# A decoder block with a mixture of experts on one core: the sums of a gate rearranged between VectorE and TensorE, and the loads of a branch's body issued by GpSimd

## The chip, the cores and the metric

The kernel runs on one core of one Trainium2 chip. Times are device microseconds (us) of that core; lower is better. An execution is timed as a whole. A profiled execution has, beside its own time, a span: the time from the first to the last instruction that the profile shows.

The core has five engines with a queue each: TensorE (PE; the profile shows its weight loads apart, as PEld), VectorE (DVE), ScalarE (ACT), GpSimd (POOL) and SyncE (SP), which here only issues transfers. Sixteen DMA engines move what the queues issue.

## What is computed

One block over 256 tokens of width 1024, one sequence, fp32. From a conditioning vector c comes a row of six modulation vectors:

```
mod = silu(c) @ w_ada + b_ada;  sh1, sc1, ga1, sh2, sc2, ga2 = split(mod, 6)     # 1024 each
h = rms_norm(x) * (1 + sc1) + sh1
q, k, v, xb, bg, cg, gates = split(h @ w_in)                                     # 3 x 512, 3 x 512, 2 x 1024
y_a = causal attention(q, k, v);  y_b = bg * (conv3(cg * xb) + b)
x = x + ga1 * ((sigmoid(gate_a) * (y_a @ w_pa) + sigmoid(gate_b) * (y_b @ w_pb)) @ w_o)
h2 = rms_norm(x) * (1 + sc2) + sh2
x = x + ga2 * moe(h2)       # top group of 4, top 2 of its 8 experts; silu(h2 @ w1) * (h2 @ w3) @ w2
```

What the change touches is how ga1 and ga2 (the gates of the two halves of the block), and beside them sh2 and sc2 (the second norm's shift and scale), come to be: each is silu(c) times 1024 columns of w_ada plus a row of b_ada.

## The kernel before

**Two parts.** Up to about 226 us runs the front: modulation, projections, attention, convolution, output. Behind it run the experts, in eight groups of four experts, each 32 tokens at most for an expert; all weights of all experts are loaded, 24 MB a group.

**The stream of weights.** Everything large comes through one list, `stream`, of 1 MB transfers (qkv: 768 KB): first the front's, in the order of `FIRST` and `REST` (L40 to L44; `m2` is a piece of sh2 and sc2, `g1` of ga1, `g2` of ga2, `in` of w_in), then w_pa, w_pb and w_o, then 24 for each group of experts (`in_up_dram`, `in_down_dram`). SyncE issues them strictly in this order (`pump`, L139) into slots: twelve of the ring, two lent by the tiles for the gates, and some more from tiles that are no longer needed late in the front. A transfer waits for the last reader of its slot, and for the transfer eight places before it: these use eight semaphores in turn, `DMAHW0` to `DMAHW7`, which are called lanes here. In the front the last reader of a slot is mostly the instruction that splits it (below), and in the second part the last matmul on it.

**The front's units.** w_in, w_pa, w_pb and w_o are used in 112 units, U0 to U111, each of 128 x 512 weights: U0 to U23 qkv, to U31 cg, to U39 xb, to U47 bg, to U79 the gates, to U95 w_pa and w_pb, to U111 w_o. Each has a split: ScalarE writes the high part (L402), VectorE the low part (L403; GpSimd for U33, U37 and so on to U65), and then TensorE six or twelve matmuls (L434). The splits run three units ahead of the matmuls. The order of the instructions on every engine is the order in which the program is written: `run_units` goes from unit to unit, and behind a unit it takes one step of each side task that is then running. A task is started by `after(unit, task)` and gives up its turn at each `yield` (`yield n` for n units).

**The side tasks of this change.** `mod2_task` (from U34; sh2 and sc2) and `gate2_task` (from U63; ga2) sum on TensorE: a quarter sum (`quarter_sum`, L781) multiplies one column of silu(c) with a 128 x 512 piece and leaves the sum in 32 rows of a PSUM bank, four such sums side by side. mod2's first 16 come behind U34 to U37, its last 16 behind U49 to U52, and then four matmuls (L797) reduce them, with small VectorE operations behind (L794 to L803). `gate1_task` (from U58 for the first 512 columns, from U67 for the others; ga1) sums on VectorE: eight operations on 128 x 512 a half (`ada_sum`, L339) into `part`, which GpSimd has cleared and whose first row it has filled with the bias (`ada_bias`, L343 and L344, from U20 on), and then one matmul with ones (L776) that sums over the 128 rows. The bias of ga2 is added by two matmuls on a loaded row (L811; loaded by GpSimd at L806, from U55 on). Beside these run `attention` (GpSimd multiplies by the reciprocals of its sums at L692 and L693), the convolution (L650), and at U80 and on `pa_task` (L759 to L767), of which L767 writes the low part of the merged branches.

**The branch.** An expert with more than 32 tokens needs extra passes (`alone`). After the third group of experts `overflow` loads the count of the fullest expert into a register and jumps over the body when there is none (L1170). With these inputs the body is jumped over. It is present in the program of each engine that works in it, SyncE among them because the body's weights are loaded through it (L1150, L1159).

## Time and profile before

| | |
|---|---|
| median of three runs | 659.06 us (659.05 to 659.12) |
| the profiled execution, its own time | 660.22 us |
| its span | 658.5 us |
| its mean granted TensorE clock | 0.893 of full speed |
| busy: TensorE, VectorE, ScalarE, GpSimd | 537.1, 194.9, 146.6, 41.5 us |
| moved | 259.01 MB, mean 393 GB/s |

How to read the profile: "busy" is the time in which an engine executes; a wait is idle time before an instruction, put down to what released it ("<-"). L403 is line 403 of the kernel. Names of tiles are the program's, with buffer numbers left out: `slot` is a slot of the ring, `sthi` and `stlo` the high and low parts of a split, `ps` a PSUM bank, `sm` a small tile, `part` and `ada` the accumulators named above. A q behind an engine's name (SPq) is its sequencer, which issues transfers, jumps and waits on semaphores. PEclk is the granted clock of TensorE (1.00 is 2.4 GHz). Transfers are shown from issue to landing.

### The profile page before, as it was taken

The numbers are of one execution on the slowest core, as the hardware profiler recorded it, in microseconds if no ns is written. First come the engines' busy times: TensorE is split into PE (matmuls) and PEld (weight loads), VectorE is DVE, ScalarE is ACT, GpSimd is POOL, SyncE is SP. The second block draws the span as 40 slices with busy tenths as digits, with TensorE's granted clock in tenths as the row PEclk, the third lists the DMA queues.
The fourth block names the chain that finished last, engine by engine and source line by source line (L and its number), as shares of the span: only waits on it lengthen the run. The fifth ranks groups of instructions, "written<-read, shape, count | busy, mean of one in ns | idle before, by whom it ended". The sixth has DMA issues, their size and how long they took to land. (4 is left out here: it accounts for less than half of the span.)

```text
span 658.5 us, 11764 instructions
## 1 busy us (share of the span) xinstructions
PE 537.1 (82%) x5064; PEld 327.5 (50%) x5065; DVE 194.9 (30%) x403; ACT 146.6 (22%) x290; POOL 41.5 (6%) x60
## 2 busy tenths in 40 slices
PE   7999999999999988989585668675976875586666
PEld 6678897878998736354052116201710540061024
DVE  4686539657887412020020001001100100020002
ACT  4536456744555131010010001000000100010001
POOL 0012511600040000000000000000000000000000
PEclk9999999999999998999787888757876596897769
DMA  8999993688959999999999997999999999999997
GB/s 318 425 425 399 426 425 151 258 325 364 417 186 397 411 428 425 425 427 425 427 426 424 425 427 303 425 427 428 425 427 428 426 426 428 426 424 427 428 425 286
DMA packets 37795, 259.01 MB, mean 393 GB/s; under 512 B 4574, under 2 KB 5702, under 8 KB 7272
## 3 DMA queue, kind: packets, MB, share of 16 engines
q1 hardware_dynamic: 36136, 256.98, 94.1%
q10 hardware_dynamic: 1360, 1.05, 0.5%
q8 instruction: 42, 0.69, 0.4%
q0 software_dynamic: 240, 0.16, 0.1%
q14 instruction: 17, 0.14, 0.1%
HBM read 257.12 MB, written 1.05 MB: 392 GB/s over the span
## 5 line engine op out<-in xcount | busy, mean ns | idle before, releaser
L1073 PE MATMUL ps<-slot,xg 128*32 128x512 f32 x1024 | 161.2, 736 | 72.4 <-DMA slot<-in_up_dram 69.1
L1073 PEld LDWEIGHTS ps<-slot,xg 128*32 128x32 f32 x1024 | 26.3, 118 | 190.9 <-DMA slot<-in_up_dram 156.2
L434 PE MATMUL ps<-hbuf,sthi 128*128 128x256 f32 x512 | 94.8, 287 | 0.0
L434 PEld LDWEIGHTS ps<-hbuf,sthi 128*128 128x128 f32 x512 | 79.1, 190 | 11.4 <-ACT sthi L402 6.7
L403 DVE TENSOR_TENSOR stlo<-slot,sthi 128x512 fp32r<-128x512 f32 x100 | 72.0, 723 | 38.8 <-ACT sthi L402 37.8
L402 ACT ACTIVATE sthi<-slot 128x512 fp32r<-128x512 f32 x108 | 67.9, 630 | 63.7 <-PE ps L434 50.0
L1093 PE MATMUL ps<-slot,sl 128*32 128x128 f32 x2048 | 68.1, 288 | 16.4 <-DMA slot<-in_down_dram 11.5
L1081 DVE TENSOR_TENSOR sl<-sl,ps 128x512 f32<-128x512 f32 x8 | 5.5, 687 | 248.1 <-PE ps L1073 241.5
L434 PE MATMUL ps<-hbuf,stlo 128*128 128x256 f32 x256 | 72.2, 282 | 0.7 <-POOL stlo L403 0.7
L1093 PEld LDWEIGHTS ps<-slot,sl 128*32 128x32 f32 x2048 | 57.5, 115 | 30.3 <-DMA slot<-in_down_dram 14.3
L1060 ACT ACTIVATE GW<-ps 128x256 f32<-128x256 f32 x8 | 3.1, 384 | 226.6 <-PE ps L1059 226.6
L1101 PE MATMUL ps<-slot,GW 128*128 128x512 f32 (+1 forms) x76 | 37.4, 620 | 14.3 <-DVE slot L1099 14.3
L434 PEld LDWEIGHTS ps<-hbuf,stlo 128*128 128x128 f32 x256 | 48.5, 190 | 0.9 <-POOL stlo L403 0.9
L434 PE MATMUL ps<-sthi,hbuf 128*128 128x512 f32 x128 | 43.4, 404 | 1.1 <-ACT hbuf L536 0.9
L1040 PEld LDWEIGHTS ps<-GW,x 128*128 128x128 f32 x256 | 35.0, 220 | 7.8 <-issue 6.8
L1040 PE MATMUL ps<-GW,x 128*128 128x128 f32 x256 | 37.6, 310 | 0.6 <-DVE GW L1031 0.6
L1099 DVE TENSOR_TENSOR slot<-ps,slot 128x512 f32<-128x512 f32 (+1 forms) x19 | 11.5, 606 | 87.3 <-PE ps L1093 83.1
L434 PEld LDWEIGHTS ps<-sthi,hbuf 128*128 128x128 f32 x128 | 23.7, 188 | 8.9 <-DVE hbuf L538 1.4
L1101 PEld LDWEIGHTS ps<-slot,GW 128*128 128x128 f32 x76 | 13.7, 210 | 28.4 <-DVE slot L1099 19.2
L1046 ACT ACTIVATE xg<-ps,sm,sm 128x128 f32<-128x128 f32 x32 | 12.4, 457 | 65.9 <-PE ps L1040 65.9
L434 PE MATMUL ps<-stlo,hbuf 128*128 128x512 f32 x64 | 25.1, 392 | 0.0
L1048 DVE TENSOR_SCALAR xg<-ps,sm,sm 128x128 f32<-128x128 f32 x32 | 11.2, 403 | 36.8 <-PE ps L1040 36.8
(263 smaller groups left out, 435.4 us busy)
## 6 DMA issues: line engine op xcount, KB each, us to landing
slot<-in_up_dram SPq DMA_DIRECT2D x128, 1024.0 KB, 19.6
slot<-in_down_dram SPq DMA_DIRECT2D x64, 1024.0 KB, 19.6
slot<-in_front_dram SPq DMA_DIRECT2D x42, 1024.0 KB, 11.6
slot<-in_front_dram SPq DMA_DIRECT2D x8, 768.0 KB, 14.6
gates<-in_front_dram SPq DMA_DIRECT2D x4, 1024.0 KB, 6.9
x<-in_x_dram SPq DMA_DIRECT2D x2, 512.0 KB, 3.7
out_dram<-x ACTq DMA_DIRECT2D x1, 512.0 KB
out_dram<-x ACTq DMA_DIRECT2D x4, 128.0 KB, 1.8
```

The costliest lines, as they stand in the source:

```text
L402: S.activation(hi, src, AF.Copy)
L403: (G if i in on_pool else V).tensor_sub(lo, src, hi.bitcast(F32))
L434: PE.matmul(o, l, r, start=start and n == 0, stop=stop and n == 2, skip_group_check=True)
L1040: PE.matmul(o[:, 128 * (k % 4):128 * (k % 4) + 128], x[:, t, 128 * k:128 * k + 128], Gt[:, t, :], start=t == 0, stop=t == 1)
L1046: S.activation(xg[:, k, :], src, AF.Identity, bias=sh2[:, k:k + 1], scale=a2[:, k:k + 1])
L1048: V.tensor_scalar(xg[:, k, :], src, a2[:, k:k + 1], sh2[:, k:k + 1], op0=OP.mult, op1=OP.add)
L1060: S.activation(WT.rearrange("p t n -> p (t n)"), YC[:, :256], AF.Copy)
L1073: PE.matmul(o[js, :], xg[:, k, js], w[:, j, :], start=k == 0, stop=k == DK - 1)
L1081: V.tensor_mul(sl, sl, HB)
L1093: PE.matmul(bank[js, cs], hidT[:, k, js], w[:, 4 * j + k, :], start=k == 0, stop=k == 3, skip_group_check=True)
L1099: V.tensor_mul(ysb[:, cs], (bank or (YC, YD)[n])[:, cs], ga2[:, ns])
L1101: PE.matmul(ACC[t][n][:, cs], WT[:, t, :], ysb[:, cs], start=q == 0, stop=q == NQ - 1, skip_group_check=True)
```

## The change

- **Order of the stream.** ga1's first pieces (`g100`, `g101`) move forward, between xb and the middle of mod2. The four pieces of ga2 were cut by rows (256 rows x 1024 columns); they are now cut as ga1's (512 rows x 512 columns; `g200`, `g201` for the first 512 columns, `g210`, `g211` for the others).
- **ga1.** Its first half is summed from U37 on (`gate1_sums(0)`) and reduced behind U67; its second is summed from U67 on and reduced behind U76.
- **ga2.** Its first half is summed on VectorE, as ga1 is, from U57 on, into the tile `ada2` that mod2 has used until then; GpSimd clears this tile and loads the bias row into it; one matmul with ones reduces it into bank 1 behind U77. The second half is summed on TensorE by eight quarter sums, in two groups of four (U63 and U75) instead of the sixteen in four groups for both halves before, and its bias (loaded into `part[0]` from U69 on) is added by one matmul behind U86.
- **mod2.** Its second 16 quarter sums start one unit later (`yield 12`).
- **Later.** The squares of the second norm go to bank 7 instead of bank 1, which now holds half of ga2. Behind the first group of experts, one matmul and two copies make ga2's broadcast instead of two matmuls and two copies.
- **The branch.** The body's loads are issued by GpSimd's queue instead of SyncE's.

```
-REST = ("in00 in01 in10 m20 m21 in11 m22 m23 in20 in21 in30 m24 m25 m26 in31 m27 in40 g100 in41 g101 g20 in50 g21 "
-        "g110 in51 g111 g22 in60 g23 in61").split()
+REST = ("in00 in01 in10 m20 m21 in11 m22 m23 in20 in21 g100 in30 g101 m24 m25 m26 in31 m27 in40 g200 in41 g201 in50 "
+        "g210 in51 g110 g111 in60 g211 in61").split()
...
         elif nm[:2] == "g2":
-            i = int(nm[2])
-            f.append((f"ga2.{i}", "w_ada", 256 * i, 2, 512 * GA2, 1024))
+            piece("ada", "w_ada", GA2 + int(nm[2]), int(nm[3]))
...
+    def gate1_sums(half):
+        yield from ada_part(GA1 + half, part[half])
+
     def gate1_task(half, bank):
 
-        p = part[half]
-        yield from ada_part(GA1 + half, p)
-        yield 1
-        PE.matmul(bank, one.to_broadcast([128, 128]), p, start=True, stop=True)
+        PE.matmul(bank, one.to_broadcast([128, 128]), part[half], start=True, stop=True)
         V.tensor_copy(ga1[:, 512 * half:512 * half + 512], bank)
+        yield 1
...
             if k == 3:
                 S.activation(ada2, bank, AF.Copy)
-                yield 11
+                yield 12
...
     def gate2_bias():
-        G.dma_start(ada2[0:2, :], dram("b_ada", 512 * GA2, [[512, 2], [1, 512]]))
+        G.dma_start(part[0][0:1, :], dram("b_ada", 512 * GA2 + 512, [[512, 1], [1, 512]]))
+        yield 1
+
+    def gate2_sums(bank):
+
+        ada_bias(GA2, ada2)
+        yield 1
+        yield from ada_part(GA2, ada2)
+        yield 12
+        PE.matmul(bank, one.to_broadcast([128, 128]), ada2, start=True, stop=True)
 
     def gate2_task(bank):
 
-        for half in range(2):
-            PE.matmul(bank[64 * half:64 * half + 32, :], ident[0:2, half:half + 1].to_broadcast([2, 32]), ada2[0:2, :],
-                      start=True, stop=False, skip_group_check=True)
-        for i in range(4):
-            for kk in range(2):
-                for half in range(2):
-                    quarter_sum(f"ga2.{i}", 2 * i + kk, 2 * kk + half, 2 * half + kk, bank, i == 0 and kk == 1, i == 3)
-            release(f"ga2.{i}")
-            yield 3
+        for i in range(2):
+            for j in range(4):
+                quarter_sum(f"ada11.{i}", 4 * i + j, j, j, bank, i == 0, i == 1 and j > 0)
+            release(f"ada11.{i}")
+            yield 11
+            if i == 0:
+                yield 1
+        PE.matmul(bank[:32, :], one[0:1, :].to_broadcast([1, 32]), part[0][0:1, :], start=False, stop=True,
+                  skip_group_check=True)
...
-    after(58, lambda: gate1_task(0, B[1]))
-    after(67, lambda: gate1_task(1, B[1]))
-    after(55, lambda: iter([gate2_bias()]))
+    after(37, lambda: gate1_sums(0))
+    after(67, lambda: gate1_task(0, B[1]))
+    after(67, lambda: gate1_sums(1))
+    after(76, lambda: gate1_task(1, B[1]))
+    after(56, lambda: gate2_sums(B[1]))
+    after(69, gate2_bias)
     after(63, lambda: gate2_task(B[0]))
...
-                    SY.dma_start(ysb, of_expert("up", e0, 2 * k + m, j))
+                    G.dma_start(ysb, of_expert("up", e0, 2 * k + m, j))
...
-                    SY.dma_start(ysb, of_expert("down", e0, 4 * n + c, j))
+                    G.dma_start(ysb, of_expert("down", e0, 4 * n + c, j))
...
-            for half in range(2):
-                PE.matmul((HA, HB)[half], sel2[:, half:half + 1].to_broadcast([128, 128]), ysb, start=True, stop=True)
-                V.tensor_copy(ga2[:, 512 * half:512 * half + 512], (HA, HB)[half])
+            PE.matmul(HB, sel.to_broadcast([128, 128]), ysb, start=True, stop=True)
+            V.tensor_copy(ga2[:, :512], B[1])
+            V.tensor_copy(ga2[:, 512:], HB)
```

Lines of the changed kernel stand one lower than before's up to about L806, and twelve higher from there on: L403 becomes L402, L339 becomes L338, L1170 becomes L1182.

Where it moves instructions, the orders of three queues show it. The first is SyncE's at the end of the branch: the jump's join (L1170, now L1182) and the transfers behind it, with the semaphores that each waits for. Before:

```order
L1170 UNCONDITIONAL_BRANCH
L1170 UNCONDITIONAL_BRANCH [waits SP_sequencer_49,DMAHW0_49,DMAHW1_49,DMAHW2_49,DMAHW3_49,DMAHW4_49,DMAHW5_49,DMAHW6_49,DMAHW7_49]
L139 DMA slot_79<-in_down_dram 128x2048 [waits DMAHW7_49,PE_49]
L139 DMA slot_85<-in_down_dram 128x2048 [waits DMAHW0_49,PE_49]
L139 DMA slot_83<-in_up_dram 128x2048 [waits DMAHW1_49,PE_49]
```

And the same place now:

```order
L1182 UNCONDITIONAL_BRANCH
L1182 UNCONDITIONAL_BRANCH [waits SP_sequencer_49]
L138 DMA slot_81<-in_down_dram 128x2048 [waits DMAHW7_49,PE_49]
L138 DMA slot_83<-in_down_dram 128x2048 [waits DMAHW0_49,PE_49]
L138 DMA slot_85<-in_up_dram 128x2048 [waits DMAHW1_49,PE_49]
```

The join no longer waits for the eight lanes of the stream; the transfers behind it wait for what they waited for before. SyncE's whole list has 679 rows before and 291 now, since the body's loads have gone to GpSimd.

The second is VectorE's around U58 to U62, where low parts (`stlo`) alternate with the sums of a gate (L339, now L338) and the reciprocals of the attention's sums (L691, now L690). Before:

```order
L403 TENSOR_TENSOR stlo_107<-slot_82,sthi_103 128x512 [waits Activation_49]
L691 RECIPROCAL sm_244<-sm_244 128x8
L403 TENSOR_TENSOR stlo_108<-slot_82,sthi_104 128x512 [waits PE_49,Activation_49]
L403 TENSOR_TENSOR stlo_105<-slot_85,sthi_101 128x512 [waits DMAHW5_49,PE_49,Activation_49]
L691 RECIPROCAL sm_244<-sm_244 128x8
L339 SCALAR_TENSOR_TENSOR part_219<-slot_83,sm_181,part_219 128x512 [waits DMAHW4_49,DMASW0_49]
L403 TENSOR_TENSOR stlo_107<-slot_85,sthi_103 128x512 [waits PE_49,Activation_49]
L339 SCALAR_TENSOR_TENSOR part_219<-slot_83,sm_181,part_219 128x512 [waits DVE_49]
```

Now, with the small operations of mod2 (L794 to L803) one unit later:

```order
L803 SCALAR_TENSOR_TENSOR sm_223<-sm_223,cols_b 128x8 [waits DVE_49]
L690 RECIPROCAL sm_244<-sm_244 128x8
L402 TENSOR_TENSOR stlo_108<-slot_85,sthi_104 128x512 [waits Activation_49]
L402 TENSOR_TENSOR stlo_105<-slot_84,sthi_101 128x512 [waits DMAHW7_49,PE_49,Activation_49]
L690 RECIPROCAL sm_244<-sm_244 128x8
L338 SCALAR_TENSOR_TENSOR ada_202<-slot_86,sm_181,ada_202 128x512 [waits DMAHW6_49,DMASW6_49,Pool_49]
L338 SCALAR_TENSOR_TENSOR ada_202<-slot_86,sm_181,ada_202 128x512 [waits DVE_49]
L402 TENSOR_TENSOR stlo_107<-slot_84,sthi_103 128x512 [waits PE_49,Activation_49]
```

In the place of ga1's first sums stand ga2's, into `ada`; the first of them waits for GpSimd and for one of its loads (DMASW6), and two of them stand ahead of the next low part where one stood before.

The third is GpSimd's around the same units, with the bias row of ga2 and the attention's multiplies (L692 and L693, now L691 and L692; `qkb` for the first half of the heads, `misc` for the second). Before:

```order
L403 TENSOR_TENSOR stlo_106<-slot_82,sthi_102 128x512 [waits DMAHW3_49,PE_49,Activation_49]
L806 DMA ada_202<-in_b_ada_dram 2x512 [waits DVE_49,PE_49]
L692 TENSOR_TENSOR qkb<-qkb,sm_244 128x512 [waits DVE_49]
L693 TENSOR_TENSOR qkb<-qkb,sm_244 128x1024
L692 TENSOR_TENSOR misc<-misc,sm_244 128x512 [waits DVE_49]
L693 TENSOR_TENSOR misc<-misc,sm_244 128x1024 [waits Activation_49]
L403 TENSOR_TENSOR stlo_106<-slot_85,sthi_102 128x512 [waits DMAHW5_49,PE_49,Activation_49]
```

Now:

```order
L402 TENSOR_TENSOR stlo_106<-slot_85,sthi_102 128x512 [waits DMAHW5_49,PE_49,Activation_49]
L691 TENSOR_TENSOR qkb<-qkb,sm_244 128x512 [waits DVE_49]
L692 TENSOR_TENSOR qkb<-qkb,sm_244 128x1024
L342 MEMSET ada_202 128x512 [waits PE_49]
L343 DMA ada_202<-in_b_ada_dram 1x16x32 [waits Pool_49]
L691 TENSOR_TENSOR misc<-misc,sm_244 128x512 [waits DVE_49]
L692 TENSOR_TENSOR misc<-misc,sm_244 128x1024 [waits Activation_49]
L402 TENSOR_TENSOR stlo_106<-slot_84,sthi_102 128x512 [waits DMAHW7_49,PE_49,Activation_49]
```

The load of the bias row stood ahead of all four multiplies; it now stands between those of the two halves, with a clearing of its tile in front of it.

## Rows read from the trace of the kernel before

**Rows 1.** The page: the span; and the span in 40 equal slices, for TensorE the busy share in tenths (9 is 90% or more), and the GB/s that the DMA engines moved.

```profile
span 658.5 us, 11764 instructions
...
PE   7999999999999988989585668675976875586666
...
GB/s 318 425 425 399 426 425 151 258 325 364 417 186 397 411 428 425 425 427 425 427 426 424 425 427 303 425 427 428 425 427 428 426 426 428 426 424 427 428 425 286
```

**Rows 2.** The page's chain of work that ended last, as shares of the span by engine.

```profile
DMA 34%; PE 3%; DVE 0%; issue 0%; ACT 0%; SPq 0%; DVEq 0%
```

**Rows 3.** Stretches of the span. Columns: the stretch and its length in us, the busy us of PE, PEld, DVE, ACT and POOL with the number of instructions, the granted clock of TensorE, the busy share of the DMA engines, GB/s.

```profile
75.00:98.00 23.00, 23.00 (x196) 18.48 (x195) 7.80 (x13) 10.25 (x18) 6.25 (x8) 1.00 1.01 425
98.00:131.00 33.00, 31.30 (x256) 27.13 (x255) 26.09 (x39) 23.37 (x58) 12.91 (x9) 1.00 0.54 214
...
164.00:199.00 35.00, 35.00 (x265) 33.39 (x264) 29.63 (x49) 19.18 (x32) 6.69 (x4) 1.00 0.79 308
199.00:226.00 27.00, 26.79 (x169) 22.91 (x171) 17.93 (x46) 10.68 (x22) 0.00 (x0) 1.00 1.00 404
263.00:395.00 132.00, 98.96 (x1116) 42.64 (x1104) 12.12 (x29) 7.16 (x16) 0.00 (x0) 0.89 1.01 425
411.00:645.00 234.00, 162.77 (x1645) 64.24 (x1634) 15.93 (x33) 10.84 (x24) 0.00 (x0) 0.78 1.01 426
```

**Rows 4.** The waits of SyncE's queue: who waited for what, us in total, times, the longest.

```profile
SPq L139 <- DVE stlo L403: 93.1, 19, 17.6
...
SPq L1170 <- SPq L1170: 18.2, 7, 5.1
...
SPq L139 <- DVE hbuf L767: 3.1, 1, 3.1
```

**Rows 5.** The instructions of line 1170: engine, operation, number, duration in ns (least, median, most), the first and last start in us.

```profile
L1170 SPq EVENT_SEMAPHORE  x9: 17/17/17, 393.7 to 406.9; - x9
...
L1170 POOLq EVENT_SEMAPHORE  x1: 17/17/17, 303.6 to 303.6; - x1
...
L1170 SPq COMPARE_BRANCH  x1: 50/50/50, 388.6 to 388.6; - x1
```

**Rows 6.** The timeline around the branch, from 384 to 396 and from 405 to 410 us: start, us (of several together: from the first to the end of the last), engine, line, operation, and in brackets the idle time before it with what ended it.

```profile
384.85 2.78 SPq L139 DMA_DIRECT2D slot<-in_down_dram  x2
...
406.98 0.69 DVE L1099 TENSOR_TENSOR slot<-ps,slot 128x512 f32<-128x512 f32 x1 [4.18 <-SPq L1170]
407.07 0.81 SPq L139 DMA_DIRECT2D slot<-in_down_dram  x2
...
407.97 2.07 SPq L139 DMA_DIRECT2D slot<-in_up_dram  x4
```

**Rows 7.** The stretch of the hole in DMA, with the columns of the stretches above; then the DMA issues, with KB each and the median us from issue to landing: of the whole span, and of the one issued between 407.9 and 408.4 us.

```profile
401.00:411.00 10.00, 8.22 (x171) 6.59 (x174) 2.06 (x5) 1.51 (x4) 0.00 (x0) 1.00 0.59 226
...
slot<-in_down_dram SPq DMA_DIRECT2D x64, 1024.0 KB, 19.6
...
slot<-in_up_dram SPq DMA_DIRECT2D x1, 1024.0 KB, 10.3
```

**Rows 8.** Groups of TensorE's instructions from 60 to 200 us, forms apart: line, engine, operation, out<-in, forms, number, busy us, mean ns of one, idle before.

```profile
L781 PE MATMUL ps<-slot,sm 128*32 128x512 f32 x88 | 11.7, 604 | 1.0 <-DVE sq L650 1.0
...
L776 PE MATMUL ps<-part,one 128*128 128x512 f32 x4 | 2.0, 590 | 0.0
...
L811 PE MATMUL ps<-ada,ident 2*32 2x512 f32 x4 | 1.0, 599 | 0.0
```

**Rows 9.** All waits of TensorE from 28 to 226 us, and from its timeline the matmul that reads the low part of U62.

```profile
PE ps L781 <- DVE sq L650: 1.0, 1, 1.0
PE ps L434 <- POOL stlo L403: 0.7, 1, 0.7
...
133.70 0.28 PE L434 MATMUL ps<-hbuf,stlo 128*128 128x256 f32 x1
```

**Rows 10.** DMA issues by GpSimd (KB each, median us from issue to landing), and from GpSimd's timeline the clearing of a tile of 128 x 512.

```profile
wr<-in_w_re_dram POOLq DMA_DIRECT2D x1, 128.0 KB, 7.2
part<-in_b_ada_dram POOLq DMA_DIRECT2D x2, 2.0 KB, 5.2
...
ada<-in_b_ada_dram POOLq DMA_DIRECT2D x1, 4.0 KB, 4.7
...
49.65 0.53 POOL L343 MEMSET part<- 128x512 f32 x1 [12.47 <-PE ps L509]
```

**Rows 11.** GpSimd's timeline from 120 to 129 us, the sums of a gate on VectorE (duration in ns: least, median, most; first and last start), and from the page the low parts on VectorE (number | busy us, mean ns of one | idle before).

```profile
120.18 0.57 POOL L806 DMA_DIRECT2D ada<-in_b_ada_dram  x1 [0.54 <-PE ps L797]
121.16 1.04 POOL L692 TENSOR_TENSOR qkb<-qkb,sm 128x512 f32<-128x512 f32 x1 [0.41 <-DVE sm L691]
122.16 1.89 POOL L693 TENSOR_TENSOR qkb<-qkb,sm 128x1024 f32<-128x1024 f32 x1
125.39 1.44 POOL L692 TENSOR_TENSOR misc<-misc,sm 128x512 f32<-128x512 f32 x1 [1.34 <-DVE sm L691]
126.79 2.34 POOL L693 TENSOR_TENSOR misc<-misc,sm 128x1024 f32<-128x1024 f32 x1
...
L339 DVE SCALAR_TENSOR_TENSOR part<-slot,sm,part x16: 697/744/2376, 125.2 to 161.3; 128x512 f32<-128x512 f32 x16
...
L403 DVE TENSOR_TENSOR stlo<-slot,sthi 128x512 fp32r<-128x512 f32 x100 | 72.0, 723 | 38.8 <-ACT sthi L402 37.8
```

More of the change, by code (lines that the diff above doesn't have):

```diff
@@ L82 @@
 LAST_UP = "w3.0.7"
-LENT = ("mod2.7", "ga2.1")
+LENT = ("mod2.7", "ada11.0")
 @with_exitstack
@@ L768, in pa_task @@
         yield 1
+    def gate1_sums(half):
+        yield from ada_part(GA1 + half, part[half])
     def gate1_task(half, bank):
-        p = part[half]
-        yield from ada_part(GA1 + half, p)
+        PE.matmul(bank, one.to_broadcast([128, 128]), part[half], start=True, stop=True)
+        V.tensor_copy(ga1[:, 512 * half:512 * half + 512], bank)
         yield 1
-        PE.matmul(bank, one.to_broadcast([128, 128]), p, start=True, stop=True)
-        V.tensor_copy(ga1[:, 512 * half:512 * half + 512], bank)
     def quarter_sum(key, k, j, at, bank, start, stop):
@@ L843, in squares @@
         cs = slice(512 * n, 512 * n + 512)
-        S.activation(B[1], x[:, t, cs], AF.Square, accum_out=ss2[:, t, n:n + 1])
+        S.activation(B[7], x[:, t, cs], AF.Square, accum_out=ss2[:, t, n:n + 1])
     def transp(n, t):
```

## The prediction

> **What bounds the kernel now.** I read the page first. In its slices DMA moves some 426 GB/s almost everywhere, with three kinds of holes: the front's (slices 6 to 9 and 11, and parts of others), one in slice 24, and the two ends; TensorE's row is full in the front and only six to eight tenths behind it [rows 1]. The chain of waits ends on transfers into the ring of slots, a third of the span [rows 2]. So two different limits follow each other. Up to 199 us TensorE is busy without a gap (from 164 to 199 all of it, by the stretches) while DMA moves 308 GB/s [rows 3]: the ring is full, and SyncE waits for slots. From 226 us on DMA is full and TensorE waits for it. The waits of SyncE's queue say for whom: 93.1 us for the low parts of the weight splits (the last readers of a slot in the front), 18.2 us for its own semaphores at line 1170, 3.1 us for L767 [rows 4]; most of the others are the ordinary pace, a transfer that waits for the one eight places before it.
>
> The hand-over lies at 198.8 us: the last wait there is for the pa stage's split (L767), and behind it DMA loses little: 404 against 426 GB/s over 27 us [rows 1, 3, 4], about 1.4 us. A front that reaches this point earlier by d therefore ends the kernel earlier by d, as long as DMA has no later hole; the 24th slice is one, and whatever is saved there counts whole too, because every slice behind it but the last stands at 424 to 428 GB/s [rows 1]. A transfer that merely starts earlier inside the front counts nothing: the change brings the gates' pieces in and out of the ring sooner, which fills slices 6 and 7 and empties 8 to 11 by as much, since the number of slots that are free before L767 stays the same (66 transfers go ahead of it in both).
>
> **Part 1, the branch.** No expert overflows, so the body is jumped over. SyncE compares at 388.6 us and then executes nine semaphore instructions, from 393.7 to 406.9 us [rows 5]. In the order before, the jump's join waits for all eight lanes of the ring's own transfers. SyncE issued its last transfer at about 387.3 us and the next at 407.07 [rows 6], so the queue runs dry. Two prices. By bytes: 226 GB/s instead of 426 from 401 to 411 us [rows 7], (426 - 226) / 426 x 10 = 4.7 us. By landings: a transfer takes 19.6 us with eight in flight [rows 7], so one lands each 2.45 us; the one issued at 387.3 lands at 406.9, and the third behind it should have landed at 406.9 + 3 x 2.45 = 414.3 us; it was issued at 407.97 [rows 6] and took 10.3 [rows 7], so 418.3: 4.0 us late. The end follows landings: I take **4.2**, and keep 4.0 to 4.7. In the changed order SyncE still loads the count, compares and jumps, but its join waits for no lane. The five microseconds from compare to the first semaphore may stay; seven or eight transfers in flight (19.6 us) hide them, and without that cover they would cost some 5. GpSimd now has the joins; in before it passed its branch at 303 us, the one semaphore in 17 ns [rows 5], and its own lanes have long landed. VectorE waited 4.18 us there for SyncE [rows 6]; that goes too, and next is the landing of down weights, as in every other group.
>
> The Trainium skill, "DMA: Bandwidth & Descriptors", section "Issuing engines are not separate DMA queues", says that issuing from another engine saves only the sequencer's time to initiate a transfer. By that this part would bring 0, since none of the moved transfers is issued, and the time would be that of the second rival. The trace shows otherwise, 18.2 us of waiting at a jump [rows 4], which is no issue time.
>
> **Part 2, sums on TensorE.** Each quarter sum is two recorded matmuls and four sums lie side by side, so eight records are a group: 88 in 11.7 us [rows 8], 1.07 us a group. Of the twelve groups (one reads a lent tile, in a row of its own) gate 2's four become two (U63, U75): -2.1. The two bias rows (L811, 1.0 us together [rows 8]) become one, at most 1.0 and at least half of it. Added is one reduction like gate 1's, of which two took 2.0 us [rows 8]: +1.0. Net -2.1 + 0 + 1.0 = -1.1, with a half bias -1.6; I take **-1.2**. TensorE has no gap there, so all of it is path. Behind the first expert group one matmul less is issued; DMA covers that.
>
> **Part 3, waits of TensorE in the front.** From 28 to 226 us there are two: 1.0 us of the fifth mod2 sum for VectorE's L650, and 0.7 us for GpSimd's low part of U61 [rows 9]. The first: the sums now start one unit (1.4 us) later, but VectorE has one gate sum (0.74 [rows 11]) more ahead of L650, and between 98 and 115 us hardly a gap (26.1 us busy of 33 from 98 to 131 [rows 3]), so units 50 to 52 may each be a little short. 1.0 could become 0 or stay; I take **-0.6**. The second: GpSimd's multiplies of the second half of the heads ran while VectorE worked, 1.44 and 2.34 us [rows 11]; the first half's took 1.04 and 1.89. If VectorE stands still meanwhile (below), about 0.8 us go, and 0.8 for clearing and issuing come: with the earlier TensorE I take **-0.3**, from +0.3 to -0.7.
>
> The eight sums of gate 1's first half move from U58 to U37: eight times 0.74 = 6 us of VectorE, where it is busy 7.8 of 23 us [rows 3]; nothing waits. Gate 2's eight sums take their old place, one for one.
>
> **Part 4, the added wait.** VectorE's first gate 2 sum now needs the bias row, and GpSimd issues it only behind the multiplies of the first half of the heads and a clearing, where before the row stood ahead of the multiplies and nobody waited. By the rows: the second multiply ended at 124.05 [rows 11], +0.53 clearing [rows 10], issue at about 125.0, landing 4.7 to 5.2 us later [rows 10], so 130.0. VectorE reached the sums at 125.2 [rows 11]: about 5 us standing. Behind it are two sums (1.5) and U62's low part (0.72 [rows 11]), ready at 132.2 us. TensorE read that part at 133.70 [rows 9] and will come some 0.9 us earlier, at 132.8. So it fits by 0.6, which two half-known starts can eat. I take **+0.3**, and for the ends 0 and +1.6 (the slowest of GpSimd's loads, 7.2 us [rows 10]: ready at 134.4).
>
> **The sum.** Branch -4.2, sums -1.2, waits -0.9, added wait +0.3: -6.0 us. The profiled execution took 660.22 us (span 658.5 and 1.7 around it), 1.16 over the median of the three runs, 659.06. So 654.2 for a profiled execution, and **653.1** for the median. Ends of the terms: -4.0 - 1.1 + 0.3 + 1.6 = -3.2 without anything going well in the front, and -4.7 - 1.6 - 1.7 = -8.0 with all of it: 651.1 to 655.9.
>
> **Rivals.** *The bias row eats the front.* It lands late, VectorE's stand becomes TensorE's at U62. For it: GpSimd loads of 7.2 us exist, and DMA, half idle at 125 us before (214 GB/s [rows 3]), will have more to do there. Against: the same small rows took 5.2 us under full load [rows 10]. 1.6 to 2 us of loss leave the branch and a little: 659.06 - 4.2 - 0.2 = 654.7, say 655. Here VectorE would stand still just then, and GpSimd's issue next to a working VectorE took 0.57 us [rows 11]. The Trainium skill, "SBUF — State Buffer", section "A bandwidth-pool intuition that's wrong (but worth ruling out)", tells that a load from GpSimd's queue starves for descriptors while VectorE holds the shared port, about 3.1 us for 0.62; by it the row comes 2.5 us later and the time is this rival's.
>
> *The branch gives nothing*: SyncE stalls all the same, at the jump itself, so only the front is left: 659.06 - 1.8 = 657.3. For it: SyncE still compares, 5.1 us before the first semaphore [rows 5]. Against: 13 of the 18 us lie in the semaphores, and eight in flight cover the rest.
>
> *TensorE becomes the bound behind the front, and the kernel slower.* TensorE's granted clock is 0.89 from 263 to 395 us and 0.78 from 411 to 645 us, where it is busy 162.8 of 234 us [rows 3]. Without the pause it gets no rest of that kind. Held at 1.2 GHz (0.5) all along, its work would be 162.8 x 0.78 / 0.5 = 254 us: some 20 over the stretch, so about 653 + 20 = 673. It decides from a mean of 0.78 x 162.8 / 234 = 0.54. Against: the pause is 4 us in 400, and before it the clock was higher at a higher busy share (99 of 132 us).
>
> **How the numbers follow.** Forecast 0.66 (653.1); the bias row eats the front 0.15 (655); the branch gives nothing 0.06 (657.3); all ends at their best, or more freed than I see, 0.07 (650.5); both the branch and the front empty 0.03 (659); TensorE the bound 0.03 (673). Range 650.9 to 656.0: the forecast's own ends, rounded out by 0.2, with the late bias row inside; outside stay about 2 in 10. 0.2% is 1.3 us, what a measurement can tell from no change: faster is everything below 657.7, 0.66 + 0.15 + 0.06 + 0.07 = 0.94; same 0.03, slower 0.03.
>
> **What would show it.** Right: SyncE's waits at the branch gone from its list, slice 24 near 425 GB/s; L767's wait ending at about 197; the quarter sums with 80 records; TensorE's wait at U50 shorter; VectorE with a gap of about 5 us before its first gate 2 sum and TensorE with hardly one behind it. Wrong: a TensorE wait for a low part of over 1 us near 132 us, a hole in DMA elsewhere behind 226 us, or a clock near 0.54 at the end.

## The result, and the profile after

| | before | changed |
|---|---|---|
| median (lowest to highest) | 660.41 us (658.99 to 664.81), 18 runs | 657.16 us (654.83 to 660.48), 18 runs |
| ratio | | 0.9943, 95% interval 0.9930 to 0.9956: 3.8 us less (2.9 to 4.6) |
| the profiled execution, its span | 660.22, 658.5 us | 655.23, 653.1 us |

The kernel is faster, as forecast, but by 3.8 us and not by 6.0, and 657.16 lies above the range (650.9 to 656.0), 4.1 us over the forecast of 653.1. 1.35 us of these are the base: the prediction started from the median of three runs, 659.06, and 18 runs of the same kernel have 660.41. The rest is the change's: 2.75 us by the two medians, which lie 3.25 apart, and 2.2 by the ratio of runs made side by side. Note that the one profiled execution of the changed kernel is among its fastest: its trace alone (5.4 us less of span) would have seemed to confirm the forecast, by luck.

The page of the changed kernel: its span, and what DMA moved in 40 slices.

```profile
span 653.1 us, 11738 instructions
...
GB/s 323 426 424 399 425 426 195 360 289 382 360 169 391 407 421 424 425 427 423 427 425 422 426 425 424 427 427 427 423 429 425 426 424 427 426 426 425 429 425 245
```

Slice 24 (the first is slice 0) now reads 424 (it was 303), as forecast. The last slice reads 245 (it was 286) [rows 1]. That slice alone does not tell the kernels apart, since a second trace of the kernel before has 245 in it too; but the end of the stream is where the forecast went wrong (below).

The waits of SyncE's queue, the instructions of the jump's line on SyncE, and its issue behind the last wait of the front; then the first matmul of the front's units on TensorE.

```profile
SPq L138 <- DVE hbuf L766: 3.1, 1, 3.1
...
SPq L1182 <- SPq L1182: 0.5, 1, 0.5
```
```profile
L1182 SPq COMPARE_BRANCH  x1: 50/50/50, 385.4 to 385.4; - x1
L1182 SPq EVENT_SEMAPHORE  x1: 17/17/17, 385.9 to 385.9; - x1
```
```profile
196.57 1.28 SPq L138 DMA_DIRECT2D slot<-in_up_dram  x3
```
```profile
16.48 0.50 PE L433 MATMUL ps<-sthi,hbuf 128*128 128x512 f32 x1 [0.89 <-ACT hbuf L535]
```

At the jump SyncE waits 0.5 instead of 18.2 us [rows 4], and one semaphore follows the comparison by 0.5 us where nine followed over 18 us [rows 5]. The last two rows give a measure that I use for every trace below, the **length of the front**: from the first matmul of U0 to the issue behind the wait for L766, 196.57 - 16.48 = 180.09 us. Before it was 198.83 - 16.71 = 182.12. Two traces of one kernel agree in it to 0.03 us (branch_only below, which has the front of the kernel before, has 182.23), where whole runs differ by several us.

TensorE's groups from 60 to 200 us, and all its waits from 28 to 226 us:

```profile
L781 PE MATMUL ps<-slot,sm 128*32 128x512 f32 x80 | 10.6, 604 | 0.0
...
L775 PE MATMUL ps<-part,one 128*128 128x512 f32 x4 | 2.0, 590 | 0.0
...
L826 PE MATMUL ps<-part,one 1*32 1x512 f32 x2 | 1.0, 599 | 0.0
L815 PE MATMUL ps<-ada,one 128*128 128x512 f32 x2 | 1.0, 590 | 0.0
```
```profile
PE ps L433 <- DVE sm L801: 0.4, 1, 0.4
PE ps L433 <- DVE qkb L674: 0.3, 1, 0.3
```

80 records instead of 96 (88 and a group on a lent tile), a reduction more, and the bias at its full price [rows 8]; both old waits are gone and two small ones have come [rows 9]. VectorE's timeline at the new wait, GpSimd's load ahead of it, and TensorE's matmul on U62's low part:

```profile
125.27 0.19 DVE L690 RECIPROCAL sm<-sm 128x8 f32<-128x8 f32 x1
130.06 1.54 DVE L338 SCALAR_TENSOR_TENSOR ada<-slot,sm,ada 128x512 f32<-128x512 f32 x2 [4.60 <-POOL stlo L402]
131.51 0.68 DVE L402 TENSOR_TENSOR stlo<-slot,sthi 128x512 fp32r<-128x512 f32 x1
```
```profile
124.95 0.55 POOL L343 DMA_DIRECT2D ada<-in_b_ada_dram  x1 [0.29 <-POOL ada L342]
```
```profile
132.59 0.28 PE L433 MATMUL ps<-hbuf,stlo 128*128 128x256 f32 x1
```

VectorE stands 4.60 us. The profile puts this down to GpSimd's last work, but it was the load issued at 124.95: its last completion is at 129.97, and the sum starts at 130.06. The low part is ready at 131.51 + 0.68 = 132.19, 0.4 us before TensorE reads it.

### The profile page after: what moved, and what is told of

Same layout as the page of the kernel before. It is cut to its first block, busy times and chain, and to the rows that moved or that the text cites. A ratio compares the mean times of both kernels' runs of the same rounds, so it can differ in the third digit from the quotient of the medians.

```text
span 653.1 us, 11738 instructions
## 1 busy us (share of the span) xinstructions
PE 537.7 (82%) x5046; PEld 321.2 (49%) x5047; DVE 199.8 (31%) x411; ACT 146.6 (22%) x290; POOL 42.1 (6%) x62
## 4 chain that ended last, share of the span: by engine, by line
DMA 58%; PE 37%; DVE 2%; ACT 1%; issue 1%; SPq 0%; ACTq 0%; DVEq 0%
DMA slot<-in_up_dram 39%; PE ps L433 24%; DMA slot<-in_down_dram 18%; PE ps L1085 2%; PE ps L1052 2%; PE ps L781 2%; PE ps L1105 1%; DMA gates<-in_front_dram 1%; PE ps L523 1%; PE ps L1113 1%; PE ps L870 1%; PE ps L508 0%; PE ps L712 0%; PE ps L721 0%; PE ps L272 0%
## 5 line engine op out<-in xcount | busy, mean ns | idle before, releaser
L1085 PE MATMUL ps<-slot,xg 128*32 128x512 f32 x1024 | 171.1, 771 | 68.6 <-DMA slot<-in_up_dram 65.2
L402 DVE TENSOR_TENSOR stlo<-slot,sthi 128x512 fp32r<-128x512 f32 x100 | 71.1, 716 | 30.2 <-ACT sthi L401 29.5
L1105 PEld LDWEIGHTS ps<-slot,sl 128*32 128x32 f32 x2048 | 56.1, 114 | 30.5 <-DMA slot<-in_down_dram 14.3
L1113 PE MATMUL ps<-slot,GW 128*128 128x512 f32 (+1 forms) x76 | 35.8, 596 | 13.4 <-DVE slot L1111 13.4
L1052 PEld LDWEIGHTS ps<-GW,x 128*128 128x128 f32 x256 | 32.2, 205 | 7.8 <-issue 6.8
L1052 PE MATMUL ps<-GW,x 128*128 128x128 f32 x256 | 34.8, 295 | 0.6 <-DVE GW L1043 0.6
L1113 PEld LDWEIGHTS ps<-slot,GW 128*128 128x128 f32 x76 | 13.0, 200 | 26.5 <-DVE slot L1111 18.0
```

Of the source, the lines that this page charges most:

```text
L402: (G if i in on_pool else V).tensor_sub(lo, src, hi.bitcast(F32))
L1052: PE.matmul(o[:, 128 * (k % 4):128 * (k % 4) + 128], x[:, t, 128 * k:128 * k + 128], Gt[:, t, :], start=t == 0, stop=t == 1)
L1085: PE.matmul(o[js, :], xg[:, k, js], w[:, j, :], start=k == 0, stop=k == DK - 1)
L1105: PE.matmul(bank[js, cs], hidT[:, k, js], w[:, 4 * j + k, :], start=k == 0, stop=k == 3, skip_group_check=True)
L1113: PE.matmul(ACC[t][n][:, cs], WT[:, t, :], ysb[:, cs], start=q == 0, stop=q == NQ - 1, skip_group_check=True)
```

## The experiments

Ratios are to the kernel before, which ran beside each on the same chip (median 660.8 to 661.8 us there); "of the changed kernel" means a ratio of ratios, with 0.9943 for the changed one.

**The two halves, each alone.** The branch alone:

```
-                    SY.dma_start(ysb, of_expert(...))
+                    G.dma_start(ysb, of_expert(...))       # both loads of the body, in the kernel before
```

> The kernel before with one edit: the two loads in the branch's body are issued by GpSimd's queue. The traces before and after show the last transfer land 6.0 us earlier, 2.3 of it in the front and some 3.7 behind it, while the timed runs show only 0.9943, 3.7 us. Theory A (the parts are worth what the traces show, and the shortfall is scatter among runs: slow transfers here and there): 4.0 to 4.4 us less than before, ratio 0.9935 to 0.994; SyncE's waits at line 1170 are gone and the 24th slice stands near 425 GB/s. Theory B (the pause is in part repaid in the timed runs, so the branch is worth half): about 2 us less, ratio near 0.997. Theory C (the branch is worth its price and the front nothing): as A here, 0.994, and front_only at 1.000.

Measured 0.9963 (0.9946 to 0.9979): 2.4 us less (1.4 to 3.6). SyncE's waits at L1170 are 0.5 us and slice 24 moves 426 GB/s, so the hole is gone whole; yet the time falls by little more than half of 4.2. Theory A falls, B holds.

```profile
SPq L1170 <- SPq L1170: 0.5, 1, 0.5
```
```profile
GB/s 326 425 426 398 426 423 152 254 324 369 417 189 394 362 408 425 424 426 424 428 425 423 423 427 426 425 428 427 425 428 426 427 424 427 428 424 427 425 427 247
```

The sums alone (the changed kernel with SY in the two loads):

> The changed kernel with the branch's loads back on SyncE's queue, so that only the rearranged sums are left. Theory A: 1.8 to 2.3 us less than before, ratio 0.9965 to 0.9973, the last wait for L766 ends about 2 us earlier than before's 198.8 us, and SyncE's pause at the branch is back (18 us of waits, the hole in DMA). Theory B: the same, 0.997. Theory C: 0 to 0.5 us, ratio 0.9993 to 1.000.

Measured 0.9975 (0.9958 to 0.9992): 1.65 us less (0.5 to 2.8). The front is 196.50 - 16.39 = 180.11 us long, 2.0 less than before, and the pause is back (18.2 us of waits at L1182, 306 GB/s in slice 24). Theory C falls.

The changed kernel and the kernel before, once more each:

> The changed kernel as it is, for a second trace and a second set of times beside the two halves. Theory A: ratio 0.991 to 0.9945 and equal to the product of branch_only and front_only; the trace shows the front's 2 us, no pause, and another set of slow transfers behind 226 us than the first trace had. Theory B: 0.994, and the trace shows transfers behind the branch that land later than one each 2.45 us by some 2 us in sum. Theory C: 0.994, equal to branch_only.

> The kernel before as it is, against itself: how far two sets of runs of one kernel lie apart, and a second trace. All theories: ratio 0.998 to 1.002. Theory A: single runs scatter by several us, as the changed kernel's do (654.8 to 660.5), and the second trace shows the same front to within 0.3 us and other slow transfers behind 226 us. Theories B and C: the second trace has a shorter pause at the branch (B) or a front that is a microsecond or two shorter (C) than the first.

Measured 0.9948 (0.9926 to 0.9971) and 0.9999 (0.9983 to 1.0014). The product of the halves is 0.9938. The fronts are 180.06 and 182.14 us long, as in the first traces. What differs between two traces of one kernel lies behind the front. One place is the hand-over, where the first expert matmul starts 26.5, 27.9 or 29.3 us behind L766's wait (L767's in the kernel before; 26.5 and 27.9 both in two traces of the kernel before and in two of the changed one). The stretch from 18.8 to 25 us behind that wait in the changed kernel's two traces (columns as in [rows 3]):

```profile
215.40:221.60 6.20, 6.07 (x56) 5.72 (x53) 4.52 (x26) 0.96 (x4) 0.00 (x0) 1.00 1.02 425
```
```profile
215.60:221.80 6.20, 6.20 (x42) 6.02 (x41) 3.74 (x23) 1.01 (x4) 0.00 (x0) 0.72 1.01 427
```

The same program ran here at a granted clock of 1.00 (2.4 GHz throughout) and of 0.72 (1.2 GHz for part of it), behind the same front without a gap, and TensorE got through 56 or 42 instructions. This, and the same at the very end, is a scatter of 1 to 3 us in single runs, and it belongs to neither kernel.

**Where the branch's other half went.** The last 11 us of the stream, up to the end of its last packet; first the kernel before, then front_only, branch_only and the changed kernel (columns as in [rows 3]):

```profile
641.50:652.50 11.00, 7.82 (x147) 5.16 (x142) 2.65 (x7) 1.16 (x3) 0.00 (x0) 1.00 0.94 390
```
```profile
638.90:649.90 11.00, 8.77 (x150) 5.20 (x139) 2.16 (x5) 0.87 (x2) 0.00 (x0) 0.84 0.94 390
```
```profile
640.30:651.30 11.00, 7.72 (x141) 5.17 (x142) 2.65 (x7) 1.15 (x3) 0.00 (x0) 1.00 0.84 345
```
```profile
635.50:646.50 11.00, 8.80 (x144) 5.55 (x140) 2.20 (x6) 0.88 (x2) 0.00 (x0) 0.84 0.85 355
```

With the pause DMA is busy for 0.94 of this stretch, without it for 0.84 to 0.85. The trace has sixteen completions for each 1 MB transfer; I take one to be each DMA engine's, and a transfer to have landed with the last of them. From the first to the last completion of one transfer pass 4.3 us ahead of the pause of the kernel before, and 0.4 us behind it: in the pause all engines wait for the last one and start level again. At the last transfer of the stream it is 3.0 to 3.6 us in the three traces with the pause, and 5.9 to 8.2 in the eight without (the two of the changed kernel, branch_only, no_branch, and the four of bias_behind, mod2_early and bias_later, below). Without the pause, engines that are behind stay behind, and the others are done early at the end. So (390 - 347) / 426 x 11 = 1.1 us of what the pause cost come back as idle engines at the end (347 is the mean of four traces without a pause: 345, 355, 348, 339).

The landings say how much the branch is worth in all. From the landing of the 110th transfer from the end (at 377 to 381 us, ahead of the pause) to that of the last one pass 272.6 to 273.0 us in the three traces with the pause, and 270.2 to 270.7 in the eight without: 2.4 us, which is also the timed effect. Up to the 95th from the end, just behind the pause, it is 40.7 to 40.9 us with it and 36.8 to 37.7 without, 3.6 us by the means; from there to the end 231.9 to 232.2 with it and 232.6 to 233.7 without, so 1.2 us are given back.

To see whether a pause costs its full price where nothing is given back, and what it is:

```
-        if q == Q_OVER:
+        if q in (2, 3, 4, 5):
             overflow(q + 1)            # in the kernel before
```

> The kernel before with the branch behind the third group repeated behind the fourth, fifth and sixth (none is taken), so that SyncE drains its lanes four times instead of once. Theory P (a pause costs only the idle time of the DMA engine that is last to finish, 406.6 to some 409 us in the first trace; what the other engines idle is no loss, since without the pause they are early at the end of the stream): three more pauses at 2.4 us, 7 us more than before, ratio 1.0095 to 1.0125. Theory Q (a pause costs the 4.0 to 4.7 us of my sum, and what branch_only fell short of is given back once, at the end of the stream): 3 x 4.1 to 4.7, 12 to 14 us more, ratio 1.018 to 1.021.

Measured 1.0195 (1.0166 to 1.0225): 12.9 us more, 4.3 for each further pause (3.7 to 5.0). Theory P, which I had made of the last engine's idle time, falls; Theory Q holds. By the landings, too, a further pause costs 4.0 us (284.7 against 272.8 from the 110th transfer on, for three). The three further bodies also bring 20 packets of instructions more (79 against 59), whose part in this is not separated. The page shows four holes, and the end is fuller than before's, since the engines have started level a short while ago (2.2 us from the first to the last completion of the last transfer):

```profile
GB/s 317 425 425 399 427 397 139 243 336 375 406 195 410 397 426 425 426 425 426 428 425 422 426 425 302 423 426 416 331 423 429 342 420 425 427 337 425 428 426 292
```
```profile
655.60:666.60 11.00, 7.93 (x143) 5.38 (x144) 2.65 (x7) 1.15 (x3) 0.00 (x0) 1.00 0.99 408
```

**What puts a DMA engine behind.** The stream lands a transfer each 2.44 us, but for some steps: in branch_only three of 1.3 us, at 352, 461 and 590 us, in the kernel before 1.6 and 1.5 us at 348 and 552. Near them stand packets of the queues that the profile calls instruction: 16 KB in 0.93 us (by its size TensorE's program), and the packet of the stream behind it takes 0.8 instead of 0.31. It shows best behind the pause of the kernel before: the transfer that lands at 411.9 us has its completions 0.4 us apart, such a packet starts at 412.1, and the next transfer lands at 415.9, 1.5 us late and with its completions 2.0 us apart. In four_pauses it is the same at each pause: one landing is 2.4 to 2.5 us late, which was Theory P's price, and one of the next three by 1.3 to 1.5 us more.

```
+    def idle_code():
+        for _ in range(16):
+            V.memset(fill[0:1, 0:1], 0.0)
...
                 release(f"{nm}.{q}.{k}")
+                idle_code()            # and the same behind each w2 slot, up to the seventh group
```

> The changed kernel with 16 one-element VectorE clears of an unused tile behind each slot's matmuls in the expert groups (2944 in all), which nobody waits for. They leave the result alone and only lengthen VectorE's program. Theory R (the steps of 1.2 to 1.4 us in the stream's landings are transfers of instructions: each holds up one DMA engine, and the stream goes with the engine that was held up most): the page shows some 0.19 MB more in the instruction queues, and the time grows by 0.8 to 2.8 us, ratio 1.001 to 1.004 against the changed kernel. Theory S (the steps come from elsewhere, the memory or a refresh): the instruction bytes grow, the steps and the time stay, within 0.4 us.

Measured 1.0234 (1.0213 to 1.0255), 19 us more than the changed kernel. Not all of this is the program's transfer, for the clears were not idle after all. On the page (the changed kernel has 17 such packets, 0.14 MB), and among the waits of TensorE and of SyncE's queue from 245 to 300 us:

```profile
GB/s 312 426 425 399 426 425 208 261 354 426 278 225 426 409 425 322 349 425 427 425 424 426 424 420 425 426 425 427 423 425 426 425 416 418 413 416 423 392 330 79
...
q14 instruction: 40, 0.33, 0.1%
```
```profile
PE ps L1100 <- DVE sl L1098: 7.3, 1, 7.3
```
```profile
SPq L142 <- PE ps L1110: 29.8, 8, 13.6
```

The clears stand in VectorE's order ahead of work that TensorE waits for (L1098, behind 11 us of clears), and then SyncE waits for slots. Slices 15 and 16 move 322 and 349 GB/s, where the changed kernel has 425 and 427: about 7 of the 19 us. The other 12 are left for Theory R, which has the mechanism, but a size that is wrong by four times: there are 23 packets of 8 KB more, and the stream's landings show a step of 0.9 to 1.0 us for almost every one. Its last 13 us in 40 slices:

```profile
GB/s 176 50 25 25 25 25 25 25 25 25 25 25 50 25 25 25 25 25 25 25 25 76 25 25 25 25 25 25 50 25 25 25 25 69 372 397 372 391 63 25
```

For some 10 us DMA moves 25 GB/s, a sixteenth of 426 being 26.6 (the rise at the end is the store of the output): one DMA engine is left with its share of the stream while fifteen are done. Of the last transfer's completions fifteen come within 1.2 us, and the sixteenth 13.9 us behind the first. So all of VectorE's instructions seem to come in over this one engine, and each transfer of them delays the whole stream. The durations of TensorE's packets repeat with every eighth (0.93, 0.93, 0.92, 0.97, 0.97, 0.95, 0.88, 0.88 us and so on in the changed kernel), which suggests that they come over eight engines by turns; no run here tests it. The Trainium skill, "Runtime: NRT & Kernel Launch", section "Instruction fetch mechanics", says that crossing from one block of instructions to the next is mostly hidden. For the engine itself the trace agrees: ahead of its 2944 clears VectorE stood 2.7 us in all. For a stream that fills the DMA engines it does not: a block of 128 instructions (2944 / 23) set the landings back by 0.9 to 1.0 us.

The same clears on GpSimd (`G.memset`):

> The 2944 one-element clears of more_code on GpSimd instead of VectorE, in the same places of the program. more_code took some 19 us for about 23 more transfers of instructions of 8 KB, 0.9 us each, as if all of them came in by one and the same DMA engine, on which every transfer of the stream then waits. Theory R1 (each engine's program comes in by one DMA engine): GpSimd's costs as much, 15 to 22 us more than the changed kernel, ratio to before 1.017 to 1.028, and DMA at some 33 GB/s at the end. Theory R2 (this is VectorE's alone, the others' instructions come in by turns, as TensorE's): 1 to 3 us more, ratio to before 0.996 to 0.999.

Measured 1.0037 (1.0022 to 1.0053), 6.2 us more than the changed kernel: neither R1's 15 to 22 nor R2's 1 to 3. Here one instruction waits for a clear, 0.5 us in all, and no slice behind the front has a hole but the end. The landings show a step for most of the transfers here too, but of 0.6 to 0.7 us, and at the end one engine is left again (the stretch from 645 to 657 us in 40 slices):

```profile
GB/s 300 246 218 246 218 246 191 246 191 137 137 109 109 27 27 82 27 27 27 27 27 27 27 61 341 416 382 403 198 27 27 82 285 104 34 34 7 27 27 29
```

So this program, too, seems to come in over one engine (R1's mechanism), at a lower price. The stall behind the clears is part of the difference between the two runs; why the step for the same 8 KB is smaller here stays open.

**Does the changed branch still cost anything?**

```
-        if q == Q_OVER:
-            overflow(q + 1)            # in the changed kernel
```

> The changed kernel without the branch (left out: the extra passes for an expert with more than 32 tokens, which these inputs don't need). Theory Q, as it now stands (a pause costs some 4.2 us where it is, and 1.1 to 1.4 of them are given back at the end of the stream, where the DMA engines finish apart; nothing of the pause is left in the changed kernel): the same time as the changed kernel, ratio to it 0.999 to 1.001, and DMA 0.84 to 0.86 busy in the last 11 us of the stream. Rival (the changed branch still costs: the jump, its code, GpSimd's join): 1 us or more less than the changed kernel, ratio 0.9985 or lower.

Measured 0.9943 (0.9921 to 0.9966), the changed kernel's ratio. DMA is 0.82 busy in the same 11 us, a little under the 0.84 expected. The interval alone leaves room for 1.5 us; by the landings nothing of the branch is left to win (270.2 us from the 110th transfer on, 270.3 and 270.6 in the changed kernel's two traces).

**The front's terms.** The bias row of gate 2's first half later:

```
-        ada_bias(GA2, ada2)
         yield 1
+        ada_bias(GA2, ada2)
         yield from ada_part(GA2, ada2)
```

> The changed kernel with gate 2's bias row (clearing and load) issued behind both pairs of GpSimd's multiplies instead of between them, 4 us later. By my sum the stand of VectorE is covered by 0.6 us: a row that lands at about 134.2 instead of 130 us makes U62's low part ready at 136.4, and TensorE waits for it some 3.5 us; the last wait for L766 and U96 come 3.3 to 4 us later than in the changed kernel, ratio to it 1.005 to 1.006. Rival (VectorE's work there is not what TensorE waits for, the splits run far enough ahead): under 0.5 us.

Measured 0.9960 (0.9937 to 0.9983), and a front of 199.40 - 16.63 = 182.77 us, 2.7 longer; the time, 1.1 us more than the changed kernel's, is not clear of noise. TensorE's waits from 28 to 226 us:

```profile
PE ps L433 <- POOL stlo L402: 1.1, 1, 1.1
PE ps L433 <- DVE stlo L402: 0.7, 1, 0.7
```

The cover is as thin as the sum said, and the loss comes, but not as I had it. The row was in at 132.1 us, not at 134.2: issued 4.4 us later, it took 2.3 us less. The larger wait is for GpSimd itself, whose low part of U61 now stands behind the clearing and the issue.

mod2's second sums one unit earlier, as before (`yield 12` to `yield 11`):

> The changed kernel with mod2's second 16 sums one unit earlier, as before (yield 11). By part 3 of my sum the later start is what took away TensorE's wait of 1.0 us for VectorE's L649 at the fifth sum: the wait comes back with 0.6 to 1.0 us, and from U0 to the issue behind the last wait for L766 pass 180.7 to 181.1 us instead of 180.1. Rival (the wait went because VectorE's order ahead of it changed, whatever the start): no such wait, 180.1.

Read from the trace of a single run: a front of 197.76 - 16.95 = 180.81 us, 0.7 longer, with the wait back:

```profile
PE ps L781 <- DVE sq L649: 1.2, 1, 1.2
```

So the later start is what took this wait away.

The bias of gate 2's second half behind the front:

```
-        PE.matmul(bank[:32, :], one[0:1, :].to_broadcast([1, 32]), part[0][0:1, :], start=False, stop=True,
-                  skip_group_check=True)
...
             S.activation(ysb, B[0], AF.Copy)
+            V.tensor_add(ysb[0:1, :], ysb[0:1, :], row)     # row: loaded by GpSimd here, behind the first group
```

> The changed kernel with the bias of gate 2's second half added behind the front: the matmul on one row (1.0 us of TensorE, behind U86) is left out, and the row is loaded behind the first expert group and added there by VectorE, where DMA covers it. By the theory that in the front all TensorE work is path: U96 begins 1.0 us earlier from U0 on, the end 1.0 us earlier than the changed kernel, ratio to it 0.9985. Rival (VectorE holds that place, not TensorE): U96 begins less than 0.3 us earlier.

> The kernel bias_later once more, for the interval of its time beside the changed kernel. All TensorE work in the front is path: ratio to before 0.9920 to 0.9930, 1.0 to 1.2 us less than the changed kernel. Rival: equal to the changed kernel, 0.9945.

Measured 0.9918 (0.9892 to 0.9944) and 0.9907 (0.9885 to 0.9929); the front is 178.94 us long in one trace and 178.93 in the other, 1.15 less than the changed kernel's. It beats the kernel before, and the changed one by 1.6 and 2.4 us, of which the second is just clear of noise. So this microsecond of TensorE's work was path.

## Why the prediction was wrong

The step that failed is in the part on the branch, and in the sentence ahead of it by which the saving at the 24th slice "counts whole too": **"The end follows landings: I take 4.2"**. The place and the cause of the pause were right: the waits at the jump are gone, the hole is filled, and VectorE no longer waits there. The price at the place was nearly right, 3.6 us by the landings (the 4.2 took it that without the pause all transfers land 2.45 us apart, and that stream has steps too). But what is saved there does not count whole. The end follows the landing of the last transfer, and that follows the DMA engine that is furthest behind. The pause had also set sixteen engines level in the middle of the stream; without it they are further apart at its end, and 1.2 us of the saving are lost again on the way. So the branch is worth 2.4 us by the landings, and 2.4 (1.4 to 3.6) by the times. That transfers of instructions drive the engines apart is shown by more_code and more_code_g for two engines' programs; for TensorE's, which makes the larger steps in these kernels, it rests on the times of its packets. By the Trainium skill, "DMA: Bandwidth & Descriptors", section "Issuing engines are not separate DMA queues", as the prediction read it, the branch would have brought nothing; branch_only is against that reading.

The base was the other miss: 659.06 stood for the kernel before, with the remark that the profiled execution lay 1.16 us over it. Over 18 runs that execution is the usual one (660.22 beside 660.41) and the three runs were low. With 660.41 the forecast and its range would have been 654.4 and up to 657.4, just enough for the measured time; the forecast saving of 6.0 us would still stand against 3.8.

The rest held, by its own steps:

- What bounds the front. The front is 2.0 us shorter, and the end follows it (front_only, 1.65 us less (0.5 to 2.8)). Forecast 1.8.
- Sums on TensorE: forecast -1.2. 16 records fewer, -2.1 us, a reduction of 1.0 more, and the bias at 1.0 as before: -1.1.
- Waits: forecast -0.9; 1.7 us [rows 9] became 0.7 in two other places. mod2_early confirms the cause of the first.
- The added wait: forecast a stand of 5 us, the low part ready at 132.2, read at 132.8, a cost of 0.3 with ends 0 and 1.6. It was 4.60 us, 132.19 and 132.59, and cost nothing: the row took 5.0 us from issue to landing, as the rows had it. bias_behind shows that the cover is thin.
- The rivals: the row did not eat the front; the branch did give something (branch_only); TensorE did not become the bound, its granted clock from 411 to 645 us is 0.77 against 0.78 [rows 3], and DMA moves 424 GB/s there.

So the mis-sized term is the branch, 4.2 where it measured 2.4, and the range was too narrow twice: its ends for the branch (4.0 to 4.7) had no place for what is given back, and the base had no width although three runs stood for it.

## What to carry to other kernels

A hole in a saturated stream may cost its lost bytes only in part (here 2.4 us of 4.7): ask whether the engines that idle in it would merely have been early at the end, and follow the landings to the last one before counting the whole. A jump whose body has transfers on a queue can drain that queue although the body is never run; here an idle queue took them over at no cost that shows. Compare traces by a length inside them (the first matmul to the last wait of the front, or one landing to another): single traces told 0.7 us apart, where whole runs of one kernel lie 6 us apart. And an instruction that is added only as a load stands in its engine's order: see who waits behind it before its time is put down to anything else.

## What the runs showed of the hardware that was not expected

- An engine's program is a load on the DMA engines. 2944 one-element clears on GpSimd, for which the others wait 0.5 us in all, made the kernel 6 us longer; the landings of the stream step by 0.6 to 0.7 us at most of its transfers of 8 KB of instructions. The same clears on VectorE made it 19 us longer, about 7 of them by a stall of TensorE and SyncE, with steps of 0.9 to 1.0 us. At the end one DMA engine alone was behind there, by 13.9 us. Near packets of 16 KB, by their size TensorE's program, stand steps of 1.3 us every 110 to 130 us (branch_only).
- The sixteen DMA engines drift apart by 6 to 8 us (completions of one transfer) in a stream with eight transfers in flight; a drained queue set them level, to 0.4 us.
- The granted clock of one stretch was 1.00 in one trace and 0.72 in another, of the kernel before as of the changed one, and 0.61 in one of bias_later, each time behind TensorE work without a gap (from 150 us to that stretch).
